# A planned schedule for a hybrid RWKV-7, RG-LRU and MLA block: ranks on VectorE and ScalarE, and the last gates ahead of a product

## The chip, the cores and the metric

The kernel runs on one core of a Trainium2 chip. Its time is the device time of one execution in microseconds, the median of several runs. A core has TensorE (matrix products), VectorE, ScalarE and GpSimd (elementwise work), SyncE (which issues the DMA transfers here), an on-chip memory SBUF and the accumulators PSUM, 8 banks of which each holds 512 fp32 numbers for each of 128 partitions. In the profile PE is TensorE, PEld its loading of weights, DVE VectorE, ACT ScalarE, POOL GpSimd and SP SyncE. The engines run side by side and wait for each other by semaphores; each goes through its own instructions in the order fixed when the program is built.

## What is computed

Two layers act on 256 tokens of width 1024, in fp32. Cut to what matters:

```python
for l in range(2):
    h = rms_norm(x, norm_mix[l])
    p = h @ w_in[l]                                   # 1024 x 6304
    y_a = rwkv7_mix(p[..., :1792], ...)               # a recurrence over 256 steps, 8 heads of 64
    y_b = rglru_mix(p[..., 1792:2816], ...)           # convolution, gates, a linear scan
    y_c = mla_mix(p[..., 2816:3232], cos, sin, ...)   # latent attention, 8 heads, causal
    gates = sigmoid(p[..., 3232:] + b_gate[l])        # 3 x 1024
    proj = einsum('bsnc,ncd->bsnd', [y_a, y_b, y_c], w_branch[l])
    x = x + sum_n(gates * proj) @ w_out[l]
    x = x + memory_xattn(rms_norm(x, norm_xattn[l]), rms_norm(mem, norm_mem[l]), ...)
    x = x + swiglu(rms_norm(x, norm_ffn[l]), w1[l], w3[l], w2[l])    # hidden width 2816
```

The three branches y_a, y_b and y_c of a layer do not depend on each other. Each needs its columns of `p`, and each is multiplied by its own part of `w_branch` before it is gated and summed.

## The kernel before

**Granules.** All weights lie in DRAM in the order of use, in granules of 128 rows by 1024 columns (512 KB). `fetch` (L518) loads one on SyncE's queue into one of three `raw` slots. `prepare` splits it in two numbers of shorter mantissa: ScalarE casts `hi<-raw` (`copy`, L457), VectorE subtracts `lo<-raw,hi` (`tt`, L410); both have three slots. Activations are split the same way, and a product of 128x128 by 128x256 is three TensorE instructions (`mm`, L468): hi by hi, hi by lo, lo by hi. A granule is 24 of them. `gran_ahead` keeps three granules prepared.

**The mixing stage** of a layer is a set of generators. `large()` holds the large products, in the order of `ORDER` (L30): P0 and P1 the columns of the recurrence's two halves of heads (eight and six granules), L0 and L1 those of the recurrent unit (RG-LRU), M those of attention (MLA), then G1, G2 the gates of branches 1 and 2, B1 and B2 the products of `y_b` and `y_c` with `w_branch`, G0 the gates of branch 0, and B0 the product of `y_a`. A G is 8 granules of 24 products, each pair followed by a tanh on ScalarE; a B is 4 granules. B1 waits for `yb` (tiles `ybh`, `ybl`), B2 for `yc`, B0 for `ya`. The other generators are three chains: `recurrence()` (the RWKV part: operands, then for each half a blockwise solve and the output), `operands()` (the operands of the second half) and `others()` (for layer 0 `memory_rstd`, the mean squares of the memory tokens, which the cross-attention of both layers uses later; then the recurrent unit's two halves in `lru_gates`, and attention in `mla`). The products of the large ones go to PSUM tag `psg`, those of the recurrence to `psr` and `psw`, those of the others to `psm`, two banks each. `ya`, the recurrence's result, is complete with `yal<-y,yah`.

**The planner.** `drive` (L285) writes the order of TensorE's instructions. It keeps a model in `Plan`: the time `pe` that TensorE has reached, and when each tile is there. At every step it takes a chain whose next products are ready, if the large ones had their turn or are not ready, and otherwise the next unit of large products; if nothing is ready it moves `pe` on. `Plan.op` (L248) gives each VectorE or ScalarE operation a time: those of the large products take none of the engine in the model (`self.first`), those of the chains are put into the first gap of their engine's list, at 1.3 (VectorE) or 1.2 (ScalarE) of their measured cost.

**The order on VectorE, ScalarE and SyncE** is made by the framework when the program is built: it goes through the program with its own model of the time and lets an engine take, of what it thinks ready, the instruction that is earliest in program order. `tc.high_priority(n)` counts an instruction as n places earlier. `drive` does that with 400 for the large products' work and not at all for the chains'.

**Slots that are shared.** Tiles named `e` (L381) have 8 slots, given in turn to the convolution and the gate branch of the recurrent unit (`lru_conv`, `lru_project`, both part of the large products' generator), to `lru_gates`, `memory_rstd` and `mla`. The gates' values of G2 and G0 lie in four `th` tiles, those of G1 in `mg`.

The functions that the diff touches:

Of the kernel before, what the change touches and what calls it, by code (L numbers as in the profile page):

```python
# [26 lines left out]

ORDER = "P0 L0 L1 M P1 G1 G2 B1 B2 G0 B0".split()  # L30

SMALL, MARGIN = 2.5, 0.3
CROWD = {"DVE": 1.3, "ACT": 1.2}

P = 128
T = 256
# [169 lines left out]
class Plan:  # L206

    def __init__(self):  # L210
        self.first = False
        self.restart()

    def restart(self):
        self.pe = 0.0
        self.busy = {"DVE": [], "ACT": []}
        self.dma = 0.0
        self.there = {}
        self.read = {}
        self.slot = {}  # L220
        self.rings = {}
        self.seen = set()
# [24 lines left out]

    def op(self, eng, o, ins, fixed, rate, n=None):  # L248

        ins = [x for x in ins if hasattr(x, "tensor")]  # L250
        cost = fixed + rate * (n or free_size(o)) + 0.06 * (len(ins) > 2)
        t = max(self.when(ins), self.slot.get(o.tensor.name, 0.0))
        if self.first:
            self.done(t + cost + 0.1, o, ins)
            return
        cost *= CROWD[eng]
        q = self.busy[eng]
        while q and q[0][1] < self.pe - 30:
            q.pop(0)
        i = 0  # L260
        while i < len(q):
            if q[i][0] - t >= cost:
                break
            t = max(t, q[i][1])
            i += 1
        q.insert(i, (t, t + cost))
        self.done(t + cost + 0.1, o, ins)

    def matmul(self, o, w, x, cost):
# [8 lines left out]
def free_size(x):  # L278
    n = 1
    for d in x.shape[1:]:  # L280
        n *= d
    return n


def drive(tc, plan, main, chains):  # L285

    waits = {}

    def step(g):
        plan.first = g is main
        try:
            with tc.high_priority(400) if g is main else contextlib.nullcontext():
                waits[g] = next(g)
        except StopIteration:
            del waits[g]
        plan.first = False

    def ready(g):  # L300
        aps, names, banks = waits[g]
        if any(n not in plan.seen for n in names):
            return math.inf
        return plan.when(aps, banks) + MARGIN * (g is not main)

    for g in chains + [main]:
        step(g)
    small = 0.0
    while waits:
        go = sorted((ready(g), i) for i, g in enumerate(chains) if g in waits)  # L310
        big = ready(main) if main in waits else math.inf
        if go and go[0][0] <= plan.pe and (small < SMALL or big > plan.pe):
            t = plan.pe
            step(chains[min(i for r, i in go if r <= plan.pe)])
            small += plan.pe - t
        elif big <= plan.pe:
            step(main)
            small = 0.0
        else:
            t = min([big] + [r for r, _ in go])  # L320
            assert t < math.inf, "nothing to issue"
            plan.pe = t
# [7 lines left out]
def hybrid_block(tc, a, out, table):  # L330
# [34 lines left out]
    def sb(p, shape, tag, bufs=1, dt=F32):  # L365
        return plan.tile(p.tile(shape, dt, tag=tag, name=name(tag), bufs=bufs), (id(p), tag), bufs)
# [1244 lines left out]
    for l in range(L):  # L1611
        mp = pool("mix%d" % l)
        st = {"ya": (sb(mp, [P, 4, T], "yah", 1, F32R), sb(mp, [P, 4, T], "yal", 1, F32R))}
        mg = sb(mp, [P, KT, T], "mg")
        yb = sb(mp, [P, 4, T], "ybh", 1, F32R), sb(mp, [P, 4, T], "ybl", 1, F32R)
        yc = sb(mp, [P, 4, T], "ych", 1, F32R), sb(mp, [P, 4, T], "ycl", 1, F32R)

        def gates(n):
            th = [mg[:, j:j + 2, :] if n == 1 else sb(mp, [P, 2, T], "th", 4) for j in range(0, KT, 2)]
            for j in range(0, KT, 2):  # L1620
                yield from gate(l, n, j, h, th[j // 2])
            return th

        def branch(n, y, th):
            for j in range(0, KT, 2):
                m, t = mg[:, j:j + 2, :], th[j // 2]
                p = yield from product(l, n, j, y)
                stt(t, t, 1.0, p, ALU.add, ALU.mult)
                if n != 1:
                    add(m, m, t)  # L1630

        def memory_rstd():
            acc = Squares(mp, "th", 4)
            for k in range(0, KT, 2):
                m = e()
                load(out=m, in_=a["mem"][:, k:k + 2, :])
                acc.feed(m)
            yield need(acc.acc, banks="m")
            vcopy(rm, rstd_tok(acc.done(), D))

        def large():
            yield from rwkv_project(l, 0, h, mp, st)
            for i in range(2):
                yield from lru_project(l, i, h, st)
            yield from mla_project(l, h, mp, st)
            yield need(after=[("free", l, 0)])
            yield from rwkv_project(l, 1, h, mp, st)
            t1 = yield from gates(1)
            t2 = yield from gates(2)
            yield need(yb, after=[("y1", l, 0), ("y1", l, 1)])  # L1650
            yield from branch(1, yb, t1)
            yield need(yc, after=[("y2", l, 0), ("y2", l, 1)])
            yield from branch(2, yc, t2)
            t0 = yield from gates(0)
            yield need(st["ya"], after=[("U", l, 0), ("U", l, 1)])
            yield from branch(0, st["ya"], t0)

        ops = [{}, {}]

        def recurrence():  # L1660
            yield from rwkv_operands(l, 0, mp, st, ops[0])
            for hv in range(2):
                yield from rwkv_solve(l, hv, mp, st, ops[hv])
                yield from rwkv_output(l, hv, mp, st, ops[hv])

        def operands():
            yield need(after=[("tok", l, 0)])
            yield from rwkv_operands(l, 1, mp, st, ops[1])

        def others():  # L1670
            if l == 0:
                yield from memory_rstd()
            for i in range(2):
                yield from lru_gates(l, i, yb, st)
            yield from mla(l, mp, st, yc)

        with tc.manual_schedule(engines={mybir.EngineType.PE}):
            plan.restart()
            drive(tc, plan, large(), [recurrence(), operands(), others()])
        h = hp_pair()  # L1680
        for k in range(0, KT, 2):
            act(h[0][:, k:k + 2, :], mg[:, k:k + 2, :], AF.Copy, scale=0.5)
            stt(h[1][:, k:k + 2, :], mg[:, k:k + 2, :], 0.5, h[0][:, k:k + 2, :].bitcast(F32), ALU.mult,
                ALU.subtract)
        close()

        pp = pool("post%d" % l)
        x = load_x(pp, x_src)

        def residual(dst=None, hl=None, gain=None, acc=None):  # L1690

            def resid(j, p):
                xj = x[:, j:j + 2, :]
                add(xj, xj, p)
                if hl is not None:
                    gained(hl, xj, lambda kk: V(l, gain, kk), j)
                if acc is not None:
                    acc.feed(xj)
                if dst is not None:
                    load(out=dst[:, j:j + 2, :], in_=xj)  # L1700
            return resid

        xp = pool("xattn%d" % l)
        hx = hp_pair(xp, "x")
        acc = Squares(xp)
        resid = residual(None, hx, "norm_xattn", acc)
        for j in range(0, KT, 2):
            po = ps_g()
            for i in range(2):
                gemm_tile(po[:, i, :], gran(l, "out", j + i), h, 0, KT, i == 0)  # L1710
            resid(j, po)
        h = hp_pair()
        acc2 = Squares(pp)
        xattn(l, kf, rm, hx, acc, xp, residual(None, h, "norm_ffn", acc2))
        close()
        fp = pool("ffn%d" % l)
        last = l == L - 1
        x_src = out if last else tc.dram_tile([P, KT, T], F32, name="x_mid")
        acc = None if last else Squares(pp)
        if not last:  # L1720
            hm = memory(l + 1, pp)
        ffn(l, h, acc2, fp, residual(x_src, None, None, acc))
        if not last:
            h = normed(slices(x), rstd_bcast(rstd_tok(acc.done(), D)), lambda kk: V(l + 1, "norm_mix", kk), hp)
            kf = sb(hp, [P, 4, T], "keys")
            keys(l + 1, kf, hm, rm)
        close()
        close()
# [19 lines left out]
```

## Time and profile before

| | |
|---|---|
| median of 3 runs | 1170.11 us (1164.99 to 1170.38) |
| the profiled execution | 1170.22 us, span 1168.4 us, mean granted clock of TensorE 0.964 |
| TensorE busy | 1087.1 us, 93% of the span |
| VectorE busy | 843.6 us, 72% |
| ScalarE busy | 605.0 us, 52% |
| mixing stage of layer 0, layer 1 | up to 317.7 us; about 601 to 901.6 us |
| DMA | 175.84 MB, mean 150 GB/s |

The span runs from the first to the last instruction of the profiled execution; what the device time has beyond it lies around it. A row of windows gives, for a stretch, its length, the busy time of each engine with the number of its instructions, the granted clock of TensorE (1.00 is the upper of its two levels, 2.4 GHz; 0.50 the lower, 1.2 GHz), and the share and rate of the DMA engines. Matmuls overlap, so busy time is the union of their times and not the sum.

### The profile page before, as it was taken

What the parts mean: (1) busy time and instruction counts of PE and PEld (TensorE: products, weight loads), DVE (VectorE), ACT (ScalarE), POOL (GpSimd) and SP (SyncE); (2) the same over time, 40 slices, a digit from 0 to 9 for tenths busy, and PEclk for the clock granted to TensorE, in tenths of its full rate; (3) what the DMA queues carried; (4) which work ended last, traced back from release to release, by engine and by line L of the source; (5) the groups of instructions that cost most, each with busy time, mean ns of one, the idle gap of its engine ahead of it and who ended that gap; (6) DMA issues with size and microseconds to landing.
All of it is one profiled execution on the core that took longest, in us unless ns stands there. A gap on an engine that the chain in (4) does not pass through costs nothing.

```text
span 1168.4 us, 23622 instructions
## 1 busy us (share of the span) xinstructions
PE 1087.1 (93%) x9684; PEld 1032.7 (88%) x9684; DVE 843.6 (72%) x1696; ACT 605.0 (52%) x963; POOL 2.7 (0%) x14
## 2 busy tenths in 40 slices
PE   4897999959999999999998979999699999999998
PEld 4786999959998899999987869999599989999998
DVE  6868866866778876775478688678667867777643
ACT  5667446543565744444445674465335655444432
POOL 0000000000000000000000000000000000000000
PEclk9897999979999999999999979999699999999999
DMA  6333434323564455555664234343234635555563
GB/s 234 126 108 107 145 105 143 102 87 103 170 217 163 151 177 181 188 184 179 202 200 161 96 102 145 109 152 103 73 106 166 217 126 163 178 183 182 172 201 115
DMA packets 54459, 175.84 MB, mean 150 GB/s; under 512 B 6224, under 2 KB 9424, under 8 KB 54352
## 3 DMA queue, kind: packets, MB, share of 16 engines
q1 hardware_dynamic: 54352, 174.34, 45.7%
q8 instruction: 76, 1.25, 0.4%
q14 instruction: 31, 0.25, 0.1%
HBM read 172.22 MB, written 2.10 MB: 149 GB/s over the span
## 4 chain that ended last, share of the span: by engine, by line
PE 79%; DVE 11%; ACT 5%; issue 3%; DMA 1%; SPq 0%; DVEq 0%; ACTq 0%
PE psg L468 52%; PE psm L468 16%; PE psw L468 4%; PE psr L468 4%; DVE lo L410 4%; ACT hi L457 2%; PE psr L472 1%; ACT e L433 1%; PE psm L472 1%; DVE e L427 1%; DVE x L410 1%; ACT qd L457 1%; DVE lo L427 1%; DVE x L445 0%; DVE e L410 0%
## 5 line engine op out<-in xcount | busy, mean ns | idle before, releaser
L457 ACT CAST hi<-raw 128x1024 fp32r<-128x1024 f32 (+1 forms) x308 | 319.0, 1036 | 374.2 <-PE psg L468 250.9
L410 DVE TENSOR_TENSOR lo<-raw,hi 128x1024 fp32r<-128x1024 f32 (+1 forms) x308 | 372.3, 1209 | 170.8 <-ACT hi L457 168.8
L468 PE MATMUL psg<-hi,hi 128*128 128x256 f32 x1280 | 376.3, 294 | 2.8 <-ACT hi L433 2.8
L468 PE MATMUL psg<-lo,hi 128*128 128x256 f32 x1280 | 366.7, 287 | 2.1 <-DVE lo L427 2.1
L468 PE MATMUL psg<-hi,lo 128*128 128x256 f32 x1280 | 366.2, 286 | 0.2
L468 PEld LDWEIGHTS psg<-hi,hi 128*128 128x128 f32 x1280 | 250.1, 195 | 10.0 <-ACT hi L433 3.9
L468 PEld LDWEIGHTS psg<-lo,hi 128*128 128x128 f32 x1280 | 250.0, 195 | 4.7 <-DVE lo L427 3.2
L468 PEld LDWEIGHTS psg<-hi,lo 128*128 128x128 f32 x1280 | 249.8, 195 | 0.7 <-DVE lo L410 0.6
L468 PE MATMUL psm<-hi,lo 128*128 128x256 f32 x352 | 99.8, 284 | 0.3 <-DVE lo L410 0.2
L468 PE MATMUL psg<-gh,hi 128*128 128x256 f32 x352 | 99.6, 283 | 0.0
L468 PE MATMUL psg<-gl,hi 128*128 128x256 f32 x352 | 99.6, 283 | 0.0
L468 PE MATMUL psg<-gh,lo 128*128 128x256 f32 x352 | 99.6, 283 | 0.0
L468 PE MATMUL psm<-hi,hi 128*128 128x256 f32 x352 | 99.6, 283 | 0.0
L468 PE MATMUL psm<-lo,hi 128*128 128x256 f32 x352 | 99.6, 283 | 0.0
L468 PEld LDWEIGHTS psm<-hi,lo 128*128 128x128 f32 x352 | 67.6, 192 | 0.7 <-DVE lo L410 0.7
L468 PEld LDWEIGHTS psg<-gh,hi 128*128 128x128 f32 x352 | 67.6, 192 | 0.0
L468 PEld LDWEIGHTS psg<-gl,hi 128*128 128x128 f32 x352 | 67.6, 192 | 0.0
L468 PEld LDWEIGHTS psg<-gh,lo 128*128 128x128 f32 x352 | 67.6, 192 | 0.0
L468 PEld LDWEIGHTS psm<-hi,hi 128*128 128x128 f32 x352 | 67.6, 192 | 0.0
L468 PEld LDWEIGHTS psm<-lo,hi 128*128 128x128 f32 x352 | 67.6, 192 | 0.0
L468 PE MATMUL psr<-x,g 64*64 64x64 f32 x256 | 12.9, 274 | 28.1 <-DVE x L445 17.3
L468 PEld LDWEIGHTS psr<-x,g 64*64 64x64 f32 x256 | 11.6, 183 | 30.0 <-DVE x L445 18.1
(364 smaller groups left out, 1763.8 us busy)
## 6 DMA issues: line engine op xcount, KB each, us to landing
raw<-in_wts SPq DMA_DIRECT2D x292, 512.0 KB, 3.5
raw<-in_wts SPq DMA_DIRECT2D x16, 384.0 KB, 4.0
e<-in_mem SPq DMA_DIRECT2D x16, 256.0 KB, 5.0
x<-in_x SPq DMA_DIRECT2D x8, 256.0 KB, 4.8
e<-in_uq SPq DMA_DIRECT2D x8, 192.0 KB, 3.8
e<-in_bd SPq DMA_DIRECT2D x4, 256.0 KB, 3.9
x_mid<-x SPq DMA_DIRECT2D x4, 256.0 KB, 4.2
x<-x_mid SPq DMA_DIRECT2D x4, 256.0 KB, 5.0
```

The costliest lines, as they stand in the source:

```text
L410: nc.vector.tensor_tensor(out=o, in0=x, in1=y, op=op)
L427: nc.vector.scalar_tensor_tensor(out=o, in0=x, scalar=s, in1=y, op0=op0, op1=op1)
L433: nc.scalar.activation(out=o, in_=x, func=f, scale=scale, bias=bias, accum_out=accum)
L457: nc.scalar.copy(out=o, in_=x)
L468: nc.tensor.matmul(o, lhsT=lhsT, rhs=rhs, start=start, stop=stop, skip_group_check=True)
L472: nc.tensor.transpose(o, x, one)
```

## The change

The order of the large products becomes G0 before B2, in the weights' order and in `large()`. The values of G0 go into two tiles with the tags of `yb` instead of `th`. Work on VectorE and ScalarE gets a rank: 0 for the large products, 1 for the recurrence and its operands, 2 for the rest. In the planner an operation sees the lists of its own and of higher ranks only, and its cost is multiplied by 1.0, 1.3 or 1.5; the large products' work now takes time in its list too. In the framework the three ranks count as 600, 300 and 0 places earlier. `memory_rstd` moves behind the first `lru_gates`.

```diff
-ORDER = "P0 L0 L1 M P1 G1 G2 B1 B2 G0 B0".split()
+ORDER = "P0 L0 L1 M P1 G1 G2 B1 G0 B2 B0".split()
...
-CROWD = {"DVE": 1.3, "ACT": 1.2}
+CROWD, RAISE = (1.0, 1.3, 1.5), (600, 300, 0)
...
-        self.busy = {"DVE": [], "ACT": []}
+        self.busy = {"DVE": [[], [], []], "ACT": [[], [], []]}
...
-        cost = fixed + rate * (n or free_size(o)) + 0.06 * (len(ins) > 2)
+        cost = (fixed + rate * (n or free_size(o)) + 0.06 * (len(ins) > 2)) * CROWD[self.rank]
         t = max(self.when(ins), self.slot.get(o.tensor.name, 0.0))
-        if self.first:
-            self.done(t + cost + 0.1, o, ins)
-            return
-        cost *= CROWD[eng]
-        q = self.busy[eng]
-        while q and q[0][1] < self.pe - 30:
-            q.pop(0)
-        i = 0
-        while i < len(q):
-            if q[i][0] - t >= cost:
+        lists = self.busy[eng]
+        for q in lists:
+            while q and q[0][1] < self.pe - 30:
+                q.pop(0)
+        for a, b in sorted(x for q in lists[:self.rank + 1] for x in q):
+            if a - t >= cost:
                 break
-            t = max(t, q[i][1])
-            i += 1
-        q.insert(i, (t, t + cost))
+            t = max(t, b)
+        lists[self.rank].append((t, t + cost))
+        lists[self.rank].sort()
         self.done(t + cost + 0.1, o, ins)
...
-        plan.first = g is main
+        plan.rank = 0 if g is main else 1 if g in chains[:2] else 2
         try:
-            with tc.high_priority(400) if g is main else contextlib.nullcontext():
+            with tc.high_priority(RAISE[plan.rank]) if RAISE[plan.rank] else contextlib.nullcontext():
...
         def gates(n):
-            th = [mg[:, j:j + 2, :] if n == 1 else sb(mp, [P, 2, T], "th", 4) for j in range(0, KT, 2)]
+            if n == 2:
+                th = [sb(mp, [P, 2, T], "th", 4) for _ in range(4)]
+            elif n == 1:
+                th = [mg[:, j:j + 2, :] for j in range(0, KT, 2)]
+            else:
+                th = [y[:, j:j + 2, :] for y in (sb(mp, [P, 4, T], n) for n in ("ybh", "ybl")) for j in (0, 2)]
...
             yield from branch(1, yb, t1)
+            t0 = yield from gates(0)
             yield need(yc, after=[("y2", l, 0), ("y2", l, 1)])
             yield from branch(2, yc, t2)
-            t0 = yield from gates(0)
             yield need(st["ya"], after=[("U", l, 0), ("U", l, 1)])
             yield from branch(0, st["ya"], t0)
...
         def others():
-            if l == 0:
-                yield from memory_rstd()
             for i in range(2):
                 yield from lru_gates(l, i, yb, st)
+                if l == 0 and i == 0:
+                    yield from memory_rstd()
             yield from mla(l, mp, st, yc)
```

## Rows read from the trace of the kernel before

**Rows 1.** The chain that ended last, by engine, shares of the span.

```profile
PE 79%; DVE 11%; ACT 5%; issue 3%; DMA 1%; SPq 0%; DVEq 0%; ACTq 0%
PE psg L468 52%; PE psm L468 16%; PE psw L468 4%; PE psr L468 4%; DVE lo L410 4%; ACT hi L457 2%; PE psr L472 1%; ACT e L433 1%; PE psm L472 1%; DVE e L427 1%; DVE x L410 1%; ACT qd L457 1%; DVE lo L427 1%; DVE x L445 0%; DVE e L410 0%
```

**Rows 2.** Windows: busy time of each engine, then clock and DMA, by stage.

```profile
28.03:39.97 11.94, 7.38 (x43) 6.08 (x43) 10.45 (x61) 7.96 (x16) 0.00 (x0) 0.71 0.34 101
39.97:115.06 75.09, 63.03 (x547) 58.95 (x546) 59.15 (x124) 51.57 (x89) 0.45 (x2) 0.89 0.37 119
115.06:236.84 121.78, 120.53 (x1273) 113.34 (x1272) 95.61 (x247) 63.97 (x122) 0.00 (x0) 1.00 0.38 122
236.84:262.00 25.16, 12.98 (x172) 10.77 (x172) 16.00 (x35) 9.97 (x23) 0.00 (x0) 0.66 0.27 85
241.35:258.42 17.07, 7.46 (x82) 6.22 (x83) 9.99 (x20) 4.53 (x11) 0.00 (x0) 0.50 0.31 96
...
640.70:698.74 58.04, 47.33 (x404) 42.90 (x405) 42.50 (x93) 40.66 (x70) 0.45 (x2) 0.82 0.33 109
818.94:844.80 25.86, 14.49 (x173) 12.03 (x173) 16.00 (x35) 9.97 (x23) 0.00 (x0) 0.60 0.25 82
821.62:842.10 20.48, 10.87 (x111) 9.02 (x112) 12.20 (x25) 6.96 (x14) 0.00 (x0) 0.50 0.31 103
```

**Rows 3.** Waits of PE from 40 to 330: us, times, longest.

```profile
PE psr L468 <- DVE x L445: 8.6, 1, 8.6
PE psr L468 <- DVE fx L410: 5.4, 1, 5.4
```

**Rows 4.** Timeline, 236 to 290: start, us, engine, line, operation [idle before].

```profile
251.29 1.97 PE L468 MATMUL psr<-x,g 64*64 64x64 f32 x32 [8.63 <-DVE x L445]
...
258.77 1.15 PE L468 MATMUL psr<-x,g 64*64 64x64 f32 x32
```

**Rows 5.** Timeline, 28 to 33.4 us: the memory's squares, lx, and PE.

```profile
31.80 0.68 DVE L410 TENSOR_TENSOR th<-th,sq 128x512 f32<-128x512 f32 x1
...
32.40 0.28 DVE L423 TENSOR_SCALAR lx<-lx 128x256 f32<-128x256 f32 x1
...
32.59 1.12 PE L468 MATMUL psm<-ones,th 128*128 128x1 f32 x7 [4.55 <-issue]
```

**Rows 6.** The chain in order of time, a piece within G0.

```profile
284.74 10.06 PE psg L468 x84
```

**Rows 7.** Timeline, 299 to 306.5 us: the end of ya, the start of B0.

```profile
299.70 0.69 DVE L410 TENSOR_TENSOR yal<-y,yah 128x512 fp32r<-128x512 f32 x1
...
306.03 0.28 PE L468 MATMUL psg<-yah,hi 128*128 128x256 f32 x1
```

**Rows 8.** The tile yal (first and last start), and B0's start in layer 1.

```profile
L410 DVE TENSOR_TENSOR yal<-y,yah x4: 682/684/686, 206.6 to 883.5; 128x512 fp32r<-128x512 f32 x4
...
889.88 0.28 PE L468 MATMUL psg<-yah,hi 128*128 128x256 f32 x1
```

**Rows 9.** Groups of DVE, 207 to 236.8 us: two of attention's.

```profile
L427 DVE SCALAR_TENSOR_TENSOR e<-psm,rn,con 128x128 f32<-128x128 f32 (+1 forms) x6 | 2.0, 387 | 0.0
L437 DVE TENSOR_REDUCE ss<-sq 128x4 f32<-128x256 f32 (+1 forms) x3 | 1.4, 463 | 0.3 <-ACT sq L433 0.2
```

**Rows 10.** Groups of DVE, 236.8 to 262 us: two of attention's.

```profile
L421 DVE TENSOR_SCALAR e<-e,sm 128x128 f32<-128x128 f32 (+1 forms) x8 | 2.3, 312 | 0.0
...
L427 DVE SCALAR_TENSOR_TENSOR e<-psm,rn,con 128x256 f32<-128x256 f32 x2 | 1.0, 481 | 0.0
```

**Rows 11.** Groups of DVE while G0 runs: count, busy, mean, idle before.

```profile
L410 DVE TENSOR_TENSOR lo<-raw,hi 128x1024 fp32r<-128x1024 f32 x8 | 9.8, 1222 | 4.6 <-ACT hi L457 4.6
```

**Rows 12.** Timeline, 92 to 96.2 us: tiles e.

```profile
92.19 0.69 DVE L427 SCALAR_TENSOR_TENSOR e<-e,e 128x512 f32<-128x512 f32 x1
...
93.94 0.62 ACT L457 COPY e<-psg 128x512 f32<-128x512 f32 x1
```

**Rows 13.** Waits of DVE from 40 to 240 us: us, times, longest.

```profile
DVE lo L410 <- ACT hi L457: 20.9, 16, 5.6
```

More of the change, by code (lines that the diff above doesn't have):

```diff
@@ L210, in __init__ @@
     def __init__(self):
-        self.first = False
+        self.rank = 2
         self.restart()
@@ L297, in step @@
             del waits[g]
-        plan.first = False
+        plan.rank = 2
     def ready(g):
```

## The prediction

> **What bounds the kernel now.** I read the chain that ended last first: 79% of it is TensorE, and more than two thirds of the span is two groups of 128x256 products [rows 1]. So only time in which TensorE stands, or runs at half its clock, can be won. The windows by stage say where that is [rows 2]. From 115.06 to 236.84 us TensorE is busy 120.53 of 121.78 us; the losses sit in three places of each mixing stage.
>
> *Between B1 and B2* (236.84 to 262.00 in layer 0): 25.16 us, TensorE busy 12.98. Inside it the granted clock is 0.50, the lower of its two levels (1.2 of 2.4 GHz), for 17.07 us with 7.46 busy [rows 2]; at the full clock that is 3.73 less. So 9.25 us of work took 25.16: 15.91 lost. Layer 1: 25.86 us, busy 14.49, of which 10.87 at half clock: 9.05 of work, 16.81 lost. The waits name the place: 8.6 us before `psr<-x,g`, a step of the recurrence's second half that waits for VectorE's `x` [rows 3]; the same 32 products take 1.97 us there and 1.15 seven us later at full clock [rows 4]. They are not the cause. The large products have only B2, which needs attention's `yc`, and G0, which needs nothing but `h`, stands behind B2 in the written order.
>
> *The front* (39.97 to 115.06): 75.09 us, busy 63.03, and by the clock's 0.89 some 16.5 us at half rate; the like holds in layer 1 (58.04, 47.33, 0.82) [rows 2]. With three quarters of the half-clock time busy (an estimate; 7.46 of 17.07 and 10.87 of 20.48 are the shares seen where the waits are longer) the loss is 12.1 + 6.2 = 18 us in layer 0 and 10.7 + 7.8 = 18.5 in layer 1. The longest wait is 5.4 us, again before a recurrence step [rows 3].
>
> *The memory's norm*, layer 0 only: 11.94 us with 7.38 busy, clock 0.71, so 6.9 us at half rate [rows 2]. One wait of 4.55 us, before `psm<-ones,th` until the sum of squares `th`, begun at 31.80, is done [rows 5], is all of the 4.56 us of idle time; the clock is lower behind it, and that time is full of work: 4.56 + 3.45 = 8.0 lost.
>
> **The change, part by part.** *G0 before B2, in both layers.* No instruction is added: 8 granules of 24 products move, with their 8 loads on SP's queue, 8 casts, 8 subtractions and 8 tanh. 84 such products took 10.06 us [rows 6], so 192 take 23.0 us: more than the 15.91 and 16.81 that are lost, so `yc` is covered even if it comes some 7 us later. The tanh go into the tiles of `yb`, free once B1 has read them; TensorE has done that by then, so this wait costs nothing (if it did: a 128x256 tanh behind one granule, under 3 us). What is late next is `ya`, because G0 was its cover. In layer 0 its last piece begins at 299.70 and takes 0.69, B0 begins at 306.03 [rows 7]: 5.65 us to spare. Layer 1: last begun at 883.5, done at 884.2, B0 at 889.88 [rows 8]: the same. With `ya` as it is, the move gives 5.65 a layer and no more; the full gain needs `ya` 10.3 and 11.2 us earlier.
>
> *Ranks.* The recurrence now goes ahead of attention and the recurrent unit on VectorE and ScalarE. What stood beside it in its second half: between 207 and 236.84 two of attention's groups take 2.0 + 1.4 us of VectorE [rows 9], which is 78% busy from 115 on (95.61 of 121.78) [rows 2], between 236.84 and 262 two take 2.3 + 1.0 [rows 10]. The half-clock passes give 2 x 0.82 = 1.6 [rows 4]. Together 8.3. Against it, G0's eight subtractions, 9.8 us in all [rows 11], now fall where the recurrence had VectorE nearly alone: half of one (0.6) for each of some eight steps is 5. That leaves 3; the recurrence's first half, which shared VectorE with both other branches, should add as much again or more. I take `ya` 7.5 us earlier, between 0 (the order hardly changes) and 16 (all of its waits behind others go). So the stretch gives 5.65 + 7.5 = **13 us a layer** (bounds 5.65 and 15.9 or 16.8). If the cover of G0 is gone, B2 waits for `yc` and each us late is a us lost.
>
> *memory_rstd behind the first lru_gates.* It adds nothing; four loads, four squares, three sums, eight products and the small operations move, and the loads pass the weights' loads on SP's queue. The 8.0 us can go, but the next step, `lora` products on `lx`, has its operand only at 32.40 + 0.28 [rows 5]; `lx` loses two 0.68 sums ahead of it. Between 0 and 8.0; I take **5**, since a half granule of large products and more stand ready. If a moved load waits for its `e` slot, weight loads queue behind it; three raw buffers cover some 8 us.
>
> *The planner counts.* Large products' VectorE and ScalarE work now fills the planner's lists, and the factors become 1.0, 1.3 and 1.5. Products of a chain that TensorE met too early (5.4, and the smaller waits of the front) are placed later, and the recurrence's are no longer queued behind the others'. This touches the 18 us of the front; no row shows how much. Between a loss of 5 and a gain of 16; I take 6, a third. Against it stands a new wait. The eight `e` slots serve the recurrent unit's first half and the large products' own second half: the ScalarE copy `e<-psg` at 93.94 takes the slot that VectorE's `e<-e,e`, begun at 92.19, frees when it ends [rows 12] (which slot, by the code). With the recurrent unit last in rank that comes later, the copy with it, and a PSUM bank of the large products is held. I charge 4 a layer (0 to 10). Net **2 a layer**.
>
> **Sum:** 2 x 13 + 5 + 2 x 2 = 35 us off the profiled execution's 1170.2 (span 1168.4 and 1.8 around it; the median of three runs is 1170.1): **1135 us**.
>
> **The rivals.** *Recurrence sets the end.* The queues' order is fixed when the program is built; a rank only prefers among what was thought ready. VectorE stood 20.9 us in front of `lo` between 40 and 240 waiting for the cast [rows 13], with whatever followed it. If a higher rank for large products only lengthens that, `ya` stays and the sum is 2 x 5.65: 1159, whatever the front gives. For it: the 5.65 us are small. Against it: attention's rows did stand in the recurrence's way [rows 9, 10]. The Trainium skill says the same of the queues ("PSUM — Partial Sum Buffer", Engine vs sequencer instructions: those of ScalarE and VectorE are strict FIFO). By that rule a rank that is wrong on the chip holds up all behind it; the row of 20.9 us agrees as far as it goes, and the time would be the 1159 just worked out.
>
> *Slots of `e` hold PSUM.* With nothing won by the planner's counting the sum is 1135 + 2 x 6 = 1147; with the new wait at 10 instead of 4 as well, 1159. For: the copy at 93.94 begins 1.06 after 92.88, when the slot comes free, with the recurrent unit still at equal rank. Against: what is left of that unit is a few operations, and VectorE has 16 us of idle time in the front (59.15 of 75.09 busy) [rows 2].
>
> *Attention comes last* (the other side). Attention is served after everything, its costs are planned at 1.5, and B2 is written before B0. For the full gain B2 must begin by 306.03 - 15.91 - 11.5 = 278.6 (half of G0's 23.0 for B2's 96 products), 16.6 us later than today (262.0, the edge of its window); the 7 us above are for B2 straight behind G0, here the recurrence's products stand between the two. Beyond that TensorE stands us for us; with B2 32 us later than now, at 294.5, the stretch gives nothing, and from there on it costs. At 40 us later in each layer it is 40 - 16.6 - 15.9 = 7.5 lost in layer 0, about 6.5 in layer 1 by the same sum, and with the 5 of the memory's norm 1170 + 14 - 5 = 1179. For: G0's splits now run on VectorE while attention ends, and recurrence and splits both go ahead. Against: the recurrence must be over before B0 too, and then only splits are ahead of attention.
>
> *The front empties as well.* If its 18 us mostly go (12 a layer instead of 2), 1135 - 20 = 1115.
>
> **How the numbers follow.** Forecast (1124 to 1146) 0.48; front empties 0.15; recurrence sets the end 0.15; slots 0.08; attention last 0.14. The range is to reach from the front's case to the recurrence's: **1111 to 1161** leaves out attention last and the outer parts of the front's and the slots' cases, 0.19 in all. 0.5% is about what a measurement of this kernel can tell from no change. Faster: 0.48 + 0.15 + 0.15 + 0.08 = 0.86. Attention last divides at B2 some 36 us later: 0.06 within 0.5%, 0.08 slower.
>
> **What the profile would show.** Right: TensorE full from B1's last product to B0's last, no clock of 0.50 there, `psr<-x,g` behind G0 products; no wait at `psm<-ones,th`; `yal` done before B0 begins. Recurrence case: TensorE idle at the end of B2 until `yal`. Slots: `psg` waiting, or idle before the MLA projections, with `e<-psg` copies late. Attention: a wait before the first `psg<-ych`. Wrong altogether if B2's or B0's wait is over 15 us.

## The result and the profile after

The changed kernel takes 1139.84 us (median of four runs, 1137.06 to 1141.23) against 1170.24 for the kernel before beside it: ratio 0.9752, 95% interval 0.971 to 0.9793. A ratio compares the means of the fast executions; one of the kernel before, at 1337.91 us, was slow and is left out of it. The forecast was 1135, the range 1111 to 1161. The profiled execution took 1141.23 us, its span 1139.5, 28.9 shorter than before; the mean granted clock rose from 0.964 to 0.982. Line numbers are one lower than before (the products are L467).

The windows by stage, first layer 0 (front, B1, from B1 to B2, B2 with B0), then layer 1 (B1, from B1 to B2, B2 with B0):

```profile
28.00:109.00 81.00, 65.56 (x570) 61.72 (x569) 66.06 (x171) 53.74 (x92) 0.45 (x2) 0.89 0.39 124
...
209.50:232.50 23.00, 22.98 (x264) 20.29 (x264) 16.83 (x31) 8.55 (x14) 0.00 (x0) 1.00 0.47 157
232.50:273.10 40.60, 39.76 (x516) 37.68 (x514) 32.46 (x89) 24.33 (x51) 0.00 (x0) 1.00 0.36 115
273.10:296.10 23.00, 23.00 (x193) 23.00 (x192) 18.55 (x24) 9.45 (x11) 0.00 (x0) 1.00 0.60 194
...
776.80:796.50 19.70, 17.02 (x138) 15.55 (x137) 13.62 (x25) 8.40 (x12) 0.00 (x0) 0.91 0.45 147
796.50:849.30 52.80, 46.58 (x614) 42.51 (x612) 35.32 (x94) 25.07 (x52) 0.00 (x0) 0.97 0.35 118
849.30:872.40 23.10, 23.10 (x193) 23.08 (x193) 19.31 (x25) 9.97 (x12) 0.00 (x0) 1.00 0.43 138
```

In layer 0 the place between B1 and B2 [rows 2] is full: 39.76 of 40.60 us busy at the upper clock level, where the stretch before had 12.98 of 25.16 and 0.66. In layer 1 6.22 us of idle time are left there, 3.6 of them at attention's transposes, and the front of layer 0 still stands 15.4 us. The longest waits of TensorE in layer 0, which answer to [rows 3], and then those of layer 1 (us in total, times, longest):

```profile
PE psm L467 <- DVE th L409: 10.5, 1, 10.5
PE psm L467 <- DVE e L426: 2.6, 1, 2.6
...
PE psm L471 <- DVE e L420: 3.6, 1, 3.6
PE psr L467 <- DVE x L444: 3.3, 1, 3.3
PE psg L467 <- ACT th L432: 2.7, 1, 2.7
PE psm L467 <- DVE t L409: 2.6, 1, 2.6
```

The two waits of 8.6 and 5.4 us at the recurrence's steps are gone from layer 0. A wait of 10.5 us at the memory's norm has come instead. The timeline from 86 to 96 us says why (start, us, what; idle before):

```profile
88.29 0.64 ACT L432 ACTIVATE sq<-e 128x512 f32<-128x512 f32 x1
...
91.40 0.68 DVE L409 TENSOR_TENSOR th<-th,sq 128x512 f32<-128x512 f32 x1
...
92.12 0.62 ACT L432 ACTIVATE sq<-e 128x512 f32<-128x512 f32 x1
...
93.15 0.68 DVE L409 TENSOR_TENSOR th<-th,sq 128x512 f32<-128x512 f32 x1
...
93.88 1.87 PE L467 MATMUL psm<-ones,th 128*128 128x1 f32 x8 [10.54 <-DVE th L409]
```

The squares and sums of a chain served last come one by one between the work of the others (each square needs the one `sq` buffer that the sum before it frees), while the eight products stand in TensorE's written order. The other engines do not stand: in a window over the wait alone VectorE is busy 10.50 of 10.54 us.

```profile
83.34:93.88 10.54, 0.00 (x1) 0.00 (x0) 10.50 (x34) 7.88 (x15) 0.00 (x0) 0.68 0.24 89
```

The last piece of `ya` and the start of B0, which answer to [rows 7, 8], first by the tile and then in the timeline:

```profile
L409 DVE TENSOR_TENSOR yal<-y,yah x4: 685/692/693, 173.4 to 850.4; 128x512 fp32r<-128x512 f32 x4
```

```profile
267.58 0.69 DVE L409 TENSOR_TENSOR yal<-y,yah 128x512 fp32r<-128x512 f32 x1
...
284.70 0.28 PE L467 MATMUL psg<-yah,hi 128*128 128x256 f32 x1
```

In layer 0 `ya` is done at 268.3 instead of 300.4, with 16.4 us to spare. All of that comes from the first half of heads: its piece, the first of the four, begins at 173.4 where it began at 206.6 [rows 8]; from the end of that piece to the end of the second half it is 94.2 us against 93.1 before.

Where the 28.9 us came from, term by term. Losses are idle time of TensorE plus half of its busy time at the lower clock level; what follows the end of layer 1's B0 takes 266.8 to 266.9 us in both kernels.

| us | predicted | measured | how |
|---|---|---|---|
| B1 to B0, layer 0 | 13 | 15.7 | 16.5 lost before (15.91 up to B2 and 0.6 in G0), 0.84 now |
| B1 to B0, layer 1 | 13 | 10.5 | 18.25 lost before (16.81 and 1.44), 7.7 now (6.2 idle, 1.5 by the clock) |
| memory's norm, where TensorE waits for it | 5 | -6.0 | 8.0 lost before; now 10.5, and 3.5 by 13.65 us at half clock with 6.98 busy |
| the rest, layer 0 | 2 | 11.6 | mixing stage ends 21.3 us earlier, less the rows above |
| the rest, layer 1 | 2 | -2.9 | from one stage's end to the next 576.2 instead of 583.8, so 7.6 less, minus 10.5 |

### The profile page after: what moved, and what is told of

Its sections match the earlier page's. It is cut to its first block, busy times and chain, and to the rows that moved or that the text cites. A ratio compares the mean times of both kernels' runs of the same rounds, so it can differ in the third digit from the quotient of the medians.

```text
span 1139.5 us, 23623 instructions
## 1 busy us (share of the span) xinstructions
PE 1078.7 (95%) x9684; PEld 1025.9 (90%) x9684; DVE 841.0 (74%) x1696; ACT 604.3 (53%) x963; POOL 2.8 (0%) x14
## 4 chain that ended last, share of the span: by engine, by line
PE 79%; DVE 11%; ACT 6%; issue 2%; DMA 1%; SPq 0%; DVEq 0%; ACTq 0%
PE psg L467 53%; PE psm L467 16%; PE psw L467 4%; DVE lo L409 4%; PE psr L467 3%; ACT hi L456 2%; PE psm L471 1%; PE psr L471 1%; DVE x L409 1%; ACT e L432 1%; ACT nb L456 1%; DVE e L426 1%; DVE lo L426 1%; ACT L432 1%; DVE e L409 0%
## 5 line engine op out<-in xcount | busy, mean ns | idle before, releaser
L467 PE MATMUL psg<-hi,hi 128*128 128x256 f32 x1280 | 375.6, 294 | 5.1 <-ACT hi L432 2.8
L467 PE MATMUL psg<-lo,hi 128*128 128x256 f32 x1280 | 366.8, 287 | 2.1 <-DVE lo L426 2.1
L467 PE MATMUL psg<-hi,lo 128*128 128x256 f32 x1280 | 366.6, 286 | 0.2
L467 PEld LDWEIGHTS psg<-hi,hi 128*128 128x128 f32 x1280 | 249.9, 195 | 12.1 <-ACT hi L432 3.9
L467 PEld LDWEIGHTS psg<-lo,hi 128*128 128x128 f32 x1280 | 250.0, 195 | 3.8 <-DVE lo L426 3.1
L467 PEld LDWEIGHTS psg<-hi,lo 128*128 128x128 f32 x1280 | 249.9, 195 | 0.7 <-DVE lo L409 0.6
L467 PE MATMUL psm<-hi,lo 128*128 128x256 f32 x352 | 99.8, 284 | 0.3 <-DVE lo L409 0.2
L467 PE MATMUL psg<-gh,hi 128*128 128x256 f32 x352 | 99.6, 283 | 0.0
L467 PE MATMUL psg<-gl,hi 128*128 128x256 f32 x352 | 99.6, 283 | 0.0
L467 PE MATMUL psg<-gh,lo 128*128 128x256 f32 x352 | 99.6, 283 | 0.0
L467 PE MATMUL psm<-hi,hi 128*128 128x256 f32 x352 | 99.6, 283 | 0.0
L467 PE MATMUL psm<-lo,hi 128*128 128x256 f32 x352 | 99.6, 283 | 0.0
L467 PEld LDWEIGHTS psm<-hi,lo 128*128 128x128 f32 x352 | 67.6, 192 | 0.7 <-DVE lo L409 0.7
L467 PEld LDWEIGHTS psg<-gh,hi 128*128 128x128 f32 x352 | 67.6, 192 | 0.0
L467 PEld LDWEIGHTS psg<-gl,hi 128*128 128x128 f32 x352 | 67.6, 192 | 0.0
L467 PEld LDWEIGHTS psg<-gh,lo 128*128 128x128 f32 x352 | 67.6, 192 | 0.0
L467 PEld LDWEIGHTS psm<-hi,hi 128*128 128x128 f32 x352 | 67.6, 192 | 0.0
L467 PEld LDWEIGHTS psm<-lo,hi 128*128 128x128 f32 x352 | 67.6, 192 | 0.0
L426 DVE SCALAR_TENSOR_TENSOR e<-e,e 128x512 f32<-128x512 f32 x42 | 28.8, 687 | 13.9 <-ACT e L432 13.2
L409 DVE TENSOR_TENSOR x<-x,psg 128x512 f32<-128x512 f32 x24 | 16.4, 684 | 11.8 <-PE psg L467 10.4
```

Of the source, the lines that this page charges most:

```text
L409: nc.vector.tensor_tensor(out=o, in0=x, in1=y, op=op)
L426: nc.vector.scalar_tensor_tensor(out=o, in0=x, scalar=s, in1=y, op0=op0, op1=op1)
L467: nc.tensor.matmul(o, lhsT=lhsT, rhs=rhs, start=start, stop=stop, skip_group_check=True)
```

## The experiments

All runs beside the kernel before of the same chip (1166 to 1170 us). "Layer 0" is the end of its last B0 product, "layer 1" the time from there to the same point of layer 1; `ya` gives the ends of the two halves' last `yal` in layer 0. Stage times are of the profiled execution (for e4 the fastest of four, 6.0 us under its median).

| kernel | median, us | ratio (95%) | layer 0 | layer 1 | `ya` |
|---|---|---|---|---|---|
| before | 1170.2 | | 317.7 | 583.8 | 207.3, 300.4 |
| changed | 1139.8 | 0.9752 (0.971 to 0.9793) | 296.4 | 576.2 | 174.1, 268.3 |
| e1_move_only | 1163.6 | 0.9954 (0.9938 to 0.997) | 315.9 | 579.0 | 206.9, 304.9 |
| e2_ranks_only | 1160.3 | 0.9933 (0.9916 to 0.995) | 307.1 | 584.0 | 171.7, 260.9 |
| e3_norm_first | 1153.0 | 0.987 (0.9851 to 0.9889) | 309.2 | 574.2 | 187.5, 287.7 |
| e4_norm_last | 1155.7 | 0.9885 (0.9852 to 0.9918) | 309.0 | 572.1 | 180.6, 279.6 |
| e5_plan_only | 1142.6 | 0.9781 (0.9755 to 0.9807) | 299.8 | 573.0 | 174.9, 271.4 |
| e6_raise_only | 1170.8 | 1.0026 (1.0009 to 1.0042) | 316.2 | 587.7 | 184.4, 303.8 |
| e7_norm_twice | 1127.2 | 0.9653 (0.9628 to 0.9678) | 295.5 | 562.8 | 173.2, 267.4 |
| e8_unit_later | 1134.2 | 0.9717 (0.9682 to 0.9751) | 304.1 | 561.2 | 166.6, 271.2 |
| e9_not_counted | 1158.1 | 0.9929 (0.9903 to 0.9955) | 311.0 | 578.5 | 151.2, 251.9 |
| e10_one_list | 1175.7 | 1.0086 (1.0059 to 1.0113) | 317.1 | 590.7 | 220.5, 306.1 |
| e11_own_chain | 1144.3 | 0.9813 (0.9786 to 0.984) | 310.3 | 563.2 | 171.5, 276.8 |
| e12_hold_layer1 | 1125.1 | 0.9653 (0.963 to 0.9676) | 294.3 | 561.3 | 172.0, 266.2 |

**The move or the ranks.** Against the kernel before, e1 has only the hunks of `ORDER`, `gates` and `large()`; against the changed kernel, e2 takes these three back (so it keeps the norm's new place too):

```diff
-ORDER = "P0 L0 L1 M P1 G1 G2 B1 G0 B2 B0".split()
+ORDER = "P0 L0 L1 M P1 G1 G2 B1 B2 G0 B0".split()
...
-            t0 = yield from gates(0)
             yield need(yc, after=[("y2", l, 0), ("y2", l, 1)])
             yield from branch(2, yc, t2)
+            t0 = yield from gates(0)
```

> The kernel before with G0 ahead of B2 alone; planner, ranks and the memory's norm as before. Theory (the move gives the cover, the ranks bring ya forward, and the two need each other): ya stays near 300 us in layer 0 and sets B0, so 5.65 us a layer, 1159 us. Rival A (the move is all of it): about 1140. Rival B (the ranks and the planner's counting are all of it): about 1170.

> The changed kernel with B2 ahead of G0 again; ranks, planner and the norm's place as changed. Theory: the recurrence ends early but nothing waits for it, and TensorE stands before B2 again, at least as long as before since attention is now last in rank: 1160 to 1172 us. Rival A (the move is all): about 1170. Rival B (ranks and counting are all): 1140 to 1148.

Alone, the move gives 4.6 us against the 1168.2 beside it and the ranks 7.9; together, by the ratio, they give 29. e1 lies between its forecasts of 1159 and about 1170. With the move alone the recurrence sets the end: in its timeline of layer 0 the product on the last `y` waits 6.2 us (the idle time ahead of it stands in brackets), and `yal` is done 4.5 us later than before; in layer 1 the like product waits 6.2 us too.

```profile
299.79 1.09 PE L472 MATMUL psr<-ident,y 128*128 128x128 f32 x4 [6.19 <-DVE y L410]
...
304.19 0.69 DVE L410 TENSOR_TENSOR yal<-y,yah 128x512 fp32r<-128x512 f32 x1 [0.74 <-ACT yah L457]
```

With the ranks alone `ya` is there at 260.9, but nobody can use it: B2 stands ahead and waits for attention, and TensorE is busy 21.45 of 30.60 us between B1 and B2 in layer 0, at a clock of 0.78. The two windows of that stretch (layer 0, layer 1):

```profile
230.20:260.80 30.60, 21.45 (x322) 17.89 (x320) 22.86 (x81) 13.71 (x35) 0.00 (x0) 0.78 0.16 56
807.90:844.80 36.90, 26.29 (x423) 21.55 (x422) 26.36 (x87) 14.61 (x37) 0.00 (x0) 0.81 0.16 57
```

**Which half of the ranks.** e5 keeps the planner's ranks and gives the framework its old priorities; e6 keeps the framework's ranks and gives the planner back its single list, its old factors, and its rule that the large products' work is not counted.

```diff
-CROWD, RAISE = (1.0, 1.3, 1.5), (600, 300, 0)
+CROWD, RAISE = (1.0, 1.3, 1.5), (400, 0, 0)
```

> The changed kernel with the framework's raise as before (400 for the large products, 0 for both kinds of chain); the planner's ranks stay. Theory (the raise brings ya forward, the planner's counting removes waits in the front): the recurrence ends 15 us or more later than in the changed kernel and B0 waits for it, 1150 to 1158. Rival (the order that the planner writes for TensorE already decides when the recurrence runs): 1138 to 1144.

> The changed kernel with the planner's model as before (large products take no time on VectorE and ScalarE, the chains share one list at 1.3 and 1.2); the raise of 600, 300 and 0 stays. Theory: ya comes early but TensorE meets chain products too early in the front, two waits of 4 us or more a layer, 1146 to 1156. Rival (the raise alone does it): 1138 to 1144.

e5 is the changed kernel within what can be told (the intervals of the ratios overlap). e6 is back at the time of before (0.26% above it), though it has the move as well. It is slower than both of its forecasts. In layer 1, which has no norm, it differs from e1 in the priorities alone and takes 587.7 us for 579.0. In layer 0 `ya`'s first half does come 23 us earlier (184.4), and it pays for that at once: TensorE meets the recurrence's steps before they are ready. Its waits in layer 0:

```profile
PE psr L471 <- DVE x L448: 11.3, 1, 11.3
...
PE psr L475 <- DVE y L413: 3.4, 1, 3.4
```

So what counts of the ranks is not the order that VectorE and ScalarE are given but the order that the planner writes for TensorE.

**Which part of the planner.** e9 leaves the large products' work uncounted again; e10 lets the recurrence see the lists of all ranks, as it did before.

```diff
+        if self.rank == 0:                       # e9
+            self.done(t + cost + 0.1, o, ins)
+            return
...
-        for a, b in sorted(x for q in lists[:self.rank + 1] for x in q):
+        for a, b in sorted(x for q in (lists if self.rank else lists[:1]) for x in q):   # e10
```

> The changed kernel, but the planner again lets the large products' VectorE and ScalarE work take no time of the engines; the chains keep their two ranks. Theory A (what matters in the planner is that the large products are counted, so that TensorE no longer meets chain products too early): back to 1155 to 1170, with waits of 4 us and more before recurrence products. Theory B (what matters is that the recurrence is planned without the other branches' work in its list): 1138 to 1146.

> The changed kernel, but in the planner the recurrence also sees the lists of attention, the recurrent unit and the norm; the large products are counted, the factors stay. Theory A: 1138 to 1146, ya's first half done near 175 us in layer 0 as in the changed kernel. Theory B: the recurrence's products are placed behind the others' work, ya's first half comes near 200 us, 1150 to 1165.

Both parts are needed, for opposite reasons; e10 is slower than either of its forecasts. Without the counting the recurrence is written too early: `ya` is whole at 251.9, but TensorE stands 11.3 us at one of its steps, and now attention comes last (its last `ycl` at 288.6, B2 begun at 287.7). Without precedence in the lists it is written too late: the first half at 220.5, the second at 306.1 in the midst of B0. The waits of layer 0 in e9:

```profile
PE psr L470 <- DVE x L447: 13.4, 2, 11.3
```

and in e10, where the norm's wait is there too:

```profile
PE psm L467 <- DVE th L409: 11.0, 1, 11.0
PE psr L471 <- DVE y L409: 6.2, 1, 6.2
PE psm L471 <- DVE e L420: 3.5, 1, 3.5
```

**The norm's wait.** e3 puts `memory_rstd` ahead of the recurrent unit as before, e4 behind attention.

```diff
         def others():
+            if l == 0:                           # e3; in e4 behind mla
+                yield from memory_rstd()
             for i in range(2):
                 yield from lru_gates(l, i, yb, st)
-                if l == 0 and i == 0:
-                    yield from memory_rstd()
             yield from mla(l, mp, st, yc)
```

> The changed kernel with memory_rstd first in its chain, as before the change. Theory (the norm's new place costs 10.5 us of waiting at 93.9 us and 3.5 at half clock, the old one cost 8.0): 6 us less, about 1134. Rival (the wait at 93.9 only stands in for another wait of the same chain): 1138 to 1142.

> The changed kernel with memory_rstd behind attention in layer 0. Theory: both prices of the norm go, 14 us less, 1126. Rival (recurrence or attention sets the end of layer 0, so that time won in the front is given back before B2 or B0): 1136 to 1142, with a new wait there.

The wait of 10.5 us is gone in both (4.9 and 5.0 remain at the norm), and both are slower than the changed kernel, and than all their forecasts; layer 0 is longer by 12.9 and 12.6 us. So something pays the wait back. In e3 the gates of the recurrent unit's second half, eight products `psm<-e,e`, begin at 89.87 and are split by a wait of 2.56:

```profile
89.87 0.67 PE L467 MATMUL psm<-e,e 128*128 128x256 f32 x2
93.09 1.94 PE L467 MATMUL psm<-e,e 128*128 128x256 f32 x6 [2.56 <-DVE t L409]
```

In the changed kernel they come behind the norm, at 112.21 in one piece; in its layer 1, which has no norm, they are split as in e3. Layer 0 and layer 1 of the timeline:

```profile
112.21 1.89 PE L467 MATMUL psm<-e,e 128*128 128x256 f32 x8
...
649.10 0.67 PE L467 MATMUL psm<-e,e 128*128 128x256 f32 x2
652.33 1.53 PE L467 MATMUL psm<-e,e 128*128 128x256 f32 x6 [2.56 <-DVE t L409]
```

Two explanations were open: TensorE's standing gives the other engines a lead, or it is the later place of the second half in the written order. e5 bears on it already. Its traced order of TensorE's products is that of the changed kernel all through layer 0's mixing, and only the priorities of the other engines' work differ; there the eight products wait for nothing, and TensorE stands in front of two of the recurrence's steps instead:

```profile
84.68 2.64 PE L467 MATMUL psw<-lx,lora 64*64 64x256 f32 x16 [5.25 <-ACT z L456]
87.25 1.86 PE L467 MATMUL psm<-ones,th 128*128 128x1 f32 x8
...
108.48 1.95 PE L467 MATMUL psr<-x,g 64*64 64x64 f32 x32 [5.16 <-DVE nrt L409]
...
112.60 1.89 PE L467 MATMUL psm<-e,e 128*128 128x256 f32 x8
```

From 28 to 109 us TensorE is busy 65.43 us in e5 and 65.56 in the changed kernel, and layer 0 ends 3.4 us later. So the wait at the norm comes of serving it last on the other engines, and without it about the same idle time stands elsewhere in the front.

e7 computes the memory's norm in both layers (`if i == 0:`), with the same values; the second time is extra work. e8 puts the norm last and holds the second half back in the written order until the solve's first inverse step of the recurrence's first half has been written:

```diff
         for u in range(8):
             for cs in HALVES:
                 mm(pn[cs, u, :], g4[cs, u, 0, :], qt[cs, u, :], u == 0, True)
+        plan.seen.add(("qt", l, hv))
...
             for i in range(2):
+                if i:                            # e12: if l and i
+                    yield need(after=[("qt", l, 0)])
                 yield from lru_gates(l, i, yb, st)
```

> The changed kernel with memory_rstd behind the first lru_gates in layer 1 too, where it only writes the same values again. Theory (without the norm's wait layer 0 took 309 us instead of 296: the wait, or the order that comes with the norm, spares later waits of attention's chain): layer 1 gains the same 10 to 13 us, 1127 to 1131. Rival (the wait costs what it shows, 10.5 us and some half clock): 1148 to 1155.

> The changed kernel with memory_rstd behind attention, and the recurrent unit's second half held back by the planner until the recurrence's solve has issued its first inverse step, in both layers; no large product is held. Theory A (what helped layer 0 is the later place of the recurrent unit's second half): layer 1 gains 10 us or more, layer 0 ends near 300 with the norm's wait in B2, 1135 to 1143 in all. Theory B (what helped is that TensorE stood still for 10 us while VectorE went on): both layers stay as with the norm last, 1150 to 1158.

With the needless norm layer 1 is 13.4 us shorter than in the changed kernel, although TensorE stands 10.6 us for it. Behind it nothing stands longer than 0.9 us, and the second half's gates are in one piece. The timeline of e7:

```profile
655.73 1.87 PE L467 MATMUL psm<-ones,th 128*128 128x1 f32 x8 [10.55 <-DVE th L409]
...
674.03 1.89 PE L467 MATMUL psm<-e,e 128*128 128x256 f32 x8
```

e8 (1134.2, just under theory A's 1135 to 1143) has no norm in layer 1 and reaches 561.2 there, so in layer 1 the norm and its standing aren't needed; the place is enough. In layer 0 e8 loses 7.7 us against the changed kernel: the norm, now last, holds TensorE in the midst of B2. Its waits in layer 0:

```profile
PE psm L467 <- DVE th L409: 6.0, 1, 6.0
PE psg L467 <- ACT th L432: 2.9, 1, 2.9
PE psr L471 <- DVE y L409: 2.9, 1, 2.9
```

**Freeing layer 0 of it.** e11 keeps e8's hold and makes the norm a chain of its own, whose products may come once the unit's second half is written.

```diff
-            yield need(acc.acc, banks="m")
+            yield need(acc.acc, banks="m", after=[("y1", l, 1)])
...
-            drive(tc, plan, large(), [recurrence(), operands(), others()])
+            drive(tc, plan, large(), [recurrence(), operands(), others()] + [memory_rstd()] * (l == 0))
```

> As e8, with memory_rstd as a chain of its own: its loads and squares begin with the layer, its products may come only when the recurrent unit's second half is done. Theory (the 6.0 us before its products in B2 and the half clock around them were the price of its place at the end): layer 0 ends near 294 instead of 304, layer 1 stays, 1123 to 1127. Rival (its early loads and squares delay the first large products as they do in the kernel before): 1129 to 1134.

This fell: 1144.3 is slower than both forecasts. The norm's products wait for nothing now, yet layer 0 ends at 310.3, where the theory had it end at about 294: attention's transposes wait instead (total, times, longest).

```profile
PE psm L471 <- DVE e L420: 10.4, 6, 4.3
PE psm L471 <- DVE ms L422: 5.8, 1, 5.8
```

The 5.8 us still hang on the norm. Its products begin at 111.33 and attention's own sums at 116.26, one to each bank of `psm`. By the code the transposes take the bank of the norm, which `ms<-psm` has to read first, and all three such operations run only from 123.25 on. First VectorE, then TensorE:

```profile
123.25 0.22 DVE L422 TENSOR_SCALAR ms<-psm 128x2 f32<-128x2 f32 x2
...
123.54 0.39 PE L471 MATMUL psm<-ident,e 32*128 32x32 f32 x2 [5.79 <-DVE ms L422]
```

In this layer 0 the second half's gates are in one piece as well (105.35), so the later place alone doesn't make a short layer.

**The hold in layer 1 alone.** e12 is the changed kernel with e8's two additions, the hold for layer 1 only.

> Layer 0 as in the changed kernel (the norm behind the recurrent unit's first half); in layer 1 alone the recurrent unit's second half is held back in the written order until the solve's first inverse step, and no norm is computed there. Theory (what pays the norm's wait back is the later place of the second half, not the norm): layer 0 ends its mixing near 296 as in the changed kernel, layer 1's stretch from end of mixing to end of mixing falls from 576 to about 561 to 563, as in the run with a second norm and in the run with the hold in both layers; span 296 + 562 + 267 = 1125, time about 1126. Rival (the gain in layer 1 needs what the other two runs changed besides, the norm itself or another layer 0): the stretch stays at 573 to 576, time 1137 to 1140.

Layer 1 takes 561.3 us and the kernel 1125.05 (five runs, 1124.17 to 1127.15): the theory's numbers. The edit is the only difference from the changed kernel. By the ratios (0.9653 and 0.9752, each against the kernel before on its chip) that is 1.0% under the changed kernel, some 11.6 us (the intervals don't meet), and 3.5% under the kernel before. The second half's gates are in one piece, 18 us later than in the changed kernel's layer 1, and the recurrence's first half ends at 729.8 instead of 749.8:

```profile
667.05 1.99 PE L467 MATMUL psm<-e,e 128*128 128x256 f32 x8
```

The longest waits that are left in layer 1:

```profile
PE psg L467 <- ACT th L432: 2.9, 1, 2.9
PE psr L471 <- DVE y L409: 2.9, 1, 2.9
PE psr L467 <- DVE x L444: 2.2, 1, 2.2
```

## Why the prediction was right, and where its steps were not

**The place of the main gain: right; its size in part by luck.** Time was lost between B1 and B2 because the large products had nothing to give there, and G0 filled it. The mean of the two layers is 13.1 us against 13 predicted, within the bounds of 5.65 and 15.9 or 16.8 in each. But it isn't 5.65 + 7.5: `ya` came earlier by more than the full gain needs in both layers. In layer 0 nearly the whole 15.9 was reached, 15.7; in layer 1, 10.5, since TensorE stands at other steps there, 3.6 us of it at attention's transposes, which the sum didn't have.

**"With `ya` as it is, the move gives 5.65 a layer and no more": shown by e1.** The move alone gave 4.6 us in all, not 11.3. In layer 1 `ya` stayed (566.4 us behind the end of layer 0's mixing, 566.5 before) and the layer got 4.8 us shorter; in layer 0 `ya` came 4.5 us later and the gain was 1.8. The second half of heads took 4.9 us longer in layer 0 and 2.4 in layer 1 (98.0 and 97.3 for 93.1 and 94.8); that fits the 5 us that the prediction charged for G0's subtractions on VectorE, but no run separates them. That the recurrence sets the end is then what the kernel does; 1163.6 was measured, and 1159 had been worked out for that rival.

**"I take `ya` 7.5 us earlier": the term was mis-sized, and its source named wrongly.** It came 32.1 and 33.2 us earlier (by clock time; 11.8 in layer 1 after its earlier start of 21.3 is taken off); 32.1 is twice the upper bound of 16. The prediction expected 3 us from the second half, where it had rows of attention's work in the recurrence's way [rows 9, 10], and the rest from the first. The second half gained nothing: 94.2 us for 93.1 in layer 0, 101.2 for 94.8 in layer 1 (749.8 to 851.0 against 789.4 to 884.2). The first half gained 33 us in layer 0 and 18 in layer 1. And it was put down to the recurrence going ahead on VectorE and ScalarE; e5 and e6 show that these priorities gain nothing here that can be measured, and that the planner's order for TensorE does it. That part of the prediction stood under "The planner counts" with 6 us a layer, 2 after the charge against it.

**The rival's ground was partly true.** The prediction warned that a higher rank for large products may only lengthen VectorE's standing in front of `lo` [rows 13]. It got shorter:

```profile
DVE lo L409 <- ACT hi L456: 14.7, 17, 2.2
```

But on ScalarE the order does hold work up once: B1's second granule in layer 1 waits 2.7 us for a `tanh` that, in ScalarE's order, stood behind four copies of the recurrence, and these waited for VectorE. The last product ahead of that `tanh` had ended at 776.9. The timeline of ScalarE:

```profile
778.00 2.63 ACT L456 COPY qd<-x 32x256 f32<-32x256 f32 x4 [2.98 <-DVE x L444]
...
781.60 0.83 ACT L432 ACTIVATE th<-psg,d_h_b_gate 128x256 f32<-128x256 f32 x2
```

The Trainium skill ("PSUM — Partial Sum Buffer", Engine vs sequencer instructions) says that the queues of ScalarE and VectorE are strict FIFO. These rows agree: the `tanh` ran right behind the copies and one cast, not in the last 1.1 of the 2.98 us in which ScalarE stood, when its products were done.

**"memory_rstd: I take 5": by its own wait wrong in sign.** The step that failed is "since a half granule of large products and more stand ready". They did (by the timeline a granule's subtraction ended at 86.4 and the last read of `psg` at 87.3), but TensorE's order is written, and the eight products stood ahead of them until 93.88: 14.0 us lost there instead of 8.0. The bounds of 0 to 8.0 had no loss in them, although the norm was now served last on both engines. And the term can't be taken by itself. The wait was paid back, since `memory_rstd` stands between the unit's two halves and moves the second to a better place: with the norm elsewhere layer 0 is 12.6 to 12.9 us longer (e3, e4), and e12 has the gain in layer 1 with no norm at all. So the norm's new place was worth about 13 us in the changed kernel, more than the 5 predicted, by a way that the prediction did not have.

**"Net 2 a layer" in the front: wrong in both layers, with opposite signs.** It was 11.6 in layer 0 and -2.9 in layer 1. The layers differ in the place of the unit's second half: held back, the layer gains (layer 0 of the changed kernel, layer 1 of e12); in layer 1 of the changed kernel it isn't, and the gain is lost. The place alone is not enough, as layer 0 of e11 shows. The charge of 4 for `e` slots had no wait to answer to: the waits for `psg` in the front of the changed kernel are two of 1.2 us in layer 0 and two of 0.6 in layer 1, and none is ended by such a copy.

**The sum** was 35 and the span lost 28.9. Predicted less measured, the terms are off by -2.7 and +2.5 (B1 to B0), +11 (norm), -9.6 and +4.9 (the rest), which makes the 6 by which the sum was too high. That the forecast came within 5 us of the median rests on these cancelling.

**Attention last** is not what sets the time, but it is near: in layer 1 of the changed kernel the last `ycl` is done at 850.3 and `ya` at 851.0, with B2 begun at 849.3, and the 3.6 us at its transposes are the longest wait of that stretch. In e9 its last work comes right in front of B2, but TensorE waits only 1.1 us there; e9's time is lost earlier, at the recurrence's steps (13.4 us in two waits).

**What stays open.** Why the two ways of taking the norm out of layer 0's front (e8 and e11) lose there is seen only by the waits, not by a run that separates them: each new written order has waits of its own elsewhere. Nor was the hold tried with other points than the solve's first inverse step, or the factors 1.0, 1.3 and 1.5 changed by themselves. That the later place helps layer 1 is shown; by which chain of waits it does so is not.

## What to carry to other kernels

Filling a hole in front of a late operand needs both the work that fills it and an earlier operand behind it; alone, the one gave a sixth and the other a quarter of what the two gave together. Where one engine's order is written from a model, try the model before the priorities of the other engines, and give it what those engines really do: here leaving out work made the order too early, counting it without precedence too late. A wait that an edit creates is no measure of the edit; compare the stage's end, and look for what else changed its place.

## What was not expected of the hardware

A needless reduction of eight 128x1 products, for which TensorE stood 10.6 us, went with a layer 13.4 us shorter. Nothing in it speeds the chip up: in the better order and without that wait e12 is only 1.5 us faster still (561.3 against 562.8). What the runs show is that a wait of TensorE can cost next to nothing. VectorE and ScalarE work on through it, as this window over e7's wait has it (VectorE 10.52 of 10.55 us), and the waits that follow in that layer then don't come: behind it none is over 0.9 us, where e12 has three of 2.2 to 2.9 us. e5 says the same from the other side: it takes the norm's wait out of layer 0 at the same order of products, and the layer is 3.4 us longer. That VectorE is what those later steps hang on fits this; no run here takes work off it.

```profile
645.18:655.73 10.55, 0.01 (x1) 0.01 (x1) 10.52 (x34) 7.88 (x15) 0.00 (x0) 0.68 0.26 89
```
